# Input, convolution and recurrence of one channel tile after another, and other places for early weights

## The chip, the cores and the metric

The kernel runs on one core of a Trainium2 chip. Its engines are TensorE (PE, with its weight loads PEld), VectorE (DVE), ScalarE (ACT), GpSimd (POOL) and SyncE (SP), which issues most DMAs. The metric is the device time of one execution in microseconds; lower is better.

## The reference, cut to what matters

One layer over 1024 latent tokens with a prefix of 256 context tokens, width 1024, all in float32.

1. adaLN: `silu(c) @ w_ada + b_ada` gives shift, scale and gate of two sublayers (for the context from `c_ctx`). `w_ada` is 1024 x 6144, 24 MB.
2. Mixer: `h = modulate(rmsnorm(x))` for latent and context tokens; one input projection with `w_in`, whose columns are q (512), k (128), v (128), the recurrence's input xr (512) and its gate branch gr (512). Group A is windowed attention with context keys. Group B is a recurrence:

```
xc = conv_b + sum_j conv_w[j] * shift(xr, j)        # width 4, latent and context apart
for d in (forward, backward):
    r, i = sigmoid(blockdiag(xc, w_r[d])), sigmoid(blockdiag(xc, w_i[d]))
    a = exp(-8 * r * softplus(-lam[d]));  b = sqrt(1 - a*a) * i * xc
    h_c = scan(a, b) over the context, from 0;  h_l = scan over the latent, from h_c's end
rnn = (h_l of both directions summed) * gelu(gr)
```

   Both groups go through `w_out`, then a gated residual.
3. A mixture of 16 experts, each of which picks 128 of the 1024 latent tokens, then a gated residual.

## The kernel before

A float32 operand is split into a high part (ScalarE copy) and the remainder (VectorE subtraction), and each product is made of three matmuls: high by high, high by remainder, remainder by high. The remainder and high part of `h` lie in SBUF as HH, HL (latent, 64 KB per partition) and CH_, CL_ (context, 16 KB).

The order of instructions is the program's, changed by a planner: it goes through the program in order of priority, places what its own cost estimates say is ready, and fills the waits of an engine with later work. The order on each engine is fixed when the kernel is built; each engine then works through its own list, with semaphores between them. Pools on the two sides of SBUF are stacks: a pool that opens after another has closed takes its space, and each tile waits only for the tiles that it overlaps.

The part that matters here, lines 208 to 624, runs in this order:

- Two context tiles of x are loaded (`load_x`), then the first third of w_ada (eight loads of 1 MB, `ada_load`, line 222): five into a ring of staging buffers, three more as slots come free, with two latent x tiles queued between. `ada_rows` (line 229) multiplies each with the conditioning vectors, four matmuls per MB. The columns of scale and shift follow (`ada_columns`), then the context's h.
- `kv_proj` makes k and v of one token tile (24 matmuls of 256 columns) with k and v's weights (`wkv`, split by `split_group`), first for the two context tiles.
- The recurrence's input has four channel tiles, 3 to 0 in order of use (`xr_weights`, line 271, splits one tile's weights; `projT`, line 281, runs them). Tile 3 is made for context and the first latent half together, then for the second half; k and v of the latent tiles stand between. The other 16 MB of w_ada are consumed by 16 calls of `ada_step` spread over these projections, through a ring of three slots; each step loads the next MB.
- Tiles 2, 1, 0 are made for the context (`xr_ctx`, line 479), the gates of adaLN are finished (`ada_gates`), and the space of CH_, CL_ and the staging goes to the recurrence's tiles.
- `conv(3)`, then for tiles 2, 1, 0 the latent projection (`xr_lat`, line 550; 48 matmuls of 512 columns) and its convolution (`conv`, line 457). `conv(t)` writes over the raw input of tile t+1.
- q's rotary tables (`rope_tables`), the router's weights and bias. Then `lru_tile` (line 508) for t = 3, 2, 1, 0: four gate products with block-diagonal weights (`gate_weights`, line 499: zeroed by VectorE, filled by four DMAs issued on POOL), tanh, exp, sqrt on ScalarE, products and three scans on VectorE. The gate tiles have four buffers, so that one tile's gates wait for the scans of the one before. Between the tiles stand five, five, five and one of the 16 steps of the query projection (24 matmuls of 256 columns each).
- The gate branch: for t = 3 to 0, 48 matmuls, gelu into a tile that lies in the recurrence's space, a product. k is stacked and transposed (`k_stack`), the eight query blocks are normalized and rotated (`norm_rope`), and attention starts (`q_stack`, `scores`).

## Time and profile before

| what | value |
|---|---|
| median of three runs | 1176.04 us (1173.61 to 1178.04) |
| the profiled execution | 1175.78 us, span 1174.0 us |
| TensorE, VectorE, ScalarE busy | 92%, 80%, 67% of the span |
| mean granted TensorE clock | 0.967 |

Times inside the profile are us from the span's start. A TensorE record lasts longer than its share of the array, because matmuls are pipelined and their ends are modelled: the distance from one start to the next is the better measure of what one costs. A granted clock of 1.00 is 2.4 GHz, and 0.50 is 1.2 GHz; values between are means over a stretch.

### The profile page before, as it was taken

The page shows a single profiled execution, that of the slowest core. Times are in us where ns is not written, and L with a number is a line of the kernel's source. Part 1 is how long each engine was busy: PE and PEld are TensorE (multiplying, and loading weights), DVE is VectorE, ACT ScalarE, POOL GpSimd, SP SyncE. Part 2 cuts the span into 40 slices and gives each one's busy share as a digit, 9 for nine tenths or more (in the row PEclk, how much of TensorE's full clock was granted, in tenths as well). Part 3 has the DMA queues.
Part 4 walks back from the last instruction along what each step waited for, and adds up shares of the span by engine and source line. Part 5 has one row for each costly group of instructions (what it writes and reads, how often), then busy time and mean ns, then how long its engine had stood idle before and what let it go on. Part 6 is the DMA issues. An engine that isn't in the chain of part 4 may idle for free.

```text
span 1174.0 us, 17069 instructions
## 1 busy us (share of the span) xinstructions
PE 1085.7 (92%) x6218; PEld 863.7 (74%) x6218; DVE 933.8 (80%) x1550; ACT 789.0 (67%) x1154; POOL 157.7 (13%) x226
## 2 busy tenths in 40 slices
PE   3999899899799999998299999999999999999995
PEld 0777678677678888786278888888888888877774
DVE  2537655778785585968888999999999999988885
ACT  2643137674475666664188888888888888897873
POOL 3015301110310000000100111101111101110001
PEclk9799899999899999999599999999999999999998
DMA  9886310102221112118799999999999999999932
GB/s 360 294 281 235 103 36 10 36 1 72 65 77 55 55 55 90 55 55 302 300 330 356 353 380 390 398 389 388 378 387 387 399 388 385 383 372 352 365 88 36
DMA packets 75636, 277.10 MB, mean 236 GB/s; under 512 B 5556, under 2 KB 12976, under 8 KB 72480
## 3 DMA queue, kind: packets, MB, share of 16 engines
q1 hardware_dynamic: 69056, 255.87, 57.3%
q0 software_dynamic: 6320, 20.07, 7.0%
q8 instruction: 49, 0.80, 0.3%
q14 instruction: 35, 0.29, 0.1%
q10 hardware_dynamic: 176, 0.07, 0.0%
HBM read 259.21 MB, written 16.79 MB: 235 GB/s over the span
## 4 chain that ended last, share of the span: by engine, by line
PE 68%; DVE 14%; ACT 7%; issue 5%; DMA 4%; POOL 2%; POOLq 0%; SPq 0%; ACTq 0%; DVEq 0%
PE pu L96 14%; PE pg L96 14%; PE pd L96 13%; PE py L96 7%; PE pxr L96 4%; PE pav L737 3%; PE pscore L96 3%; PE pPT L727 3%; DVE mlo L1090 2%; DMA wada<-in_w_ada_dram 2%; ACT gate L91 2%; PE pproj L96 1%; POOL rs L180 1%; PE pT L1131 1%; DVE gate L538 1%
## 5 line engine op out<-in xcount | busy, mean ns | idle before, releaser
L1090 DVE TENSOR_TENSOR mlo<-mraw,mhi 128x1024 fp32r<-128x1024 f32 x384 | 448.3, 1219 | 22.6 <-ACT mhi L1087 20.8
L1087 ACT ACTIVATE mhi<-mraw 128x1024 fp32r<-128x1024 f32 x384 | 397.5, 1063 | 74.2 <-PE pg L96 30.1
L96 PE MATMUL pg<-mlo,xsh 128*128 128x512 f32 x256 | 81.3, 398 | 1.4 <-DVE mlo L1090 1.4
L96 PE MATMUL pu<-mlo,xsh 128*128 128x512 f32 x256 | 80.2, 394 | 0.8 <-DVE mlo L1090 0.5
L96 PE MATMUL pu<-mhi,xsh 128*128 128x512 f32 x256 | 80.8, 390 | 0.0
L96 PE MATMUL pg<-mhi,xsh 128*128 128x512 f32 x256 | 80.5, 395 | 0.3 <-ACT xsh L1141 0.3
L96 PE MATMUL pg<-mhi,xsl 128*128 128x512 f32 x256 | 79.6, 391 | 0.0
L96 PE MATMUL pu<-mhi,xsl 128*128 128x512 f32 x256 | 79.0, 390 | 0.0
L96 PE MATMUL pd<-mlo,hdh 128*128 128x512 f32 x240 | 76.0, 398 | 2.4 <-DVE mlo L1090 2.4
L96 PE MATMUL pd<-mhi,hdh 128*128 128x512 f32 x240 | 76.4, 399 | 0.0
L96 PE MATMUL pd<-mhi,hdl 128*128 128x512 f32 x240 | 74.2, 391 | 0.0
L1118 POOL DMA_INDIRECT xs<-xh_dram,idx x16 | 22.1, 1380 | 371.5 <-ACT mhi L1087 336.5
L1180 POOL DMA_INDIRECT out_dram<-ys,idx x16 | 49.8, 3112 | 164.1 <-DVE ys L1178 164.1
L1140 ACT ACTIVATE xs<-pT,gcol 128x128 f32<-128x128 f32 x124 | 46.7, 460 | 27.1 <-PE pT L1131 27.1
L91 ACT ACTIVATE sc<-sc,mx 128x641 f32<-128x641 f32 (+1 forms) x64 | 50.9, 797 | 15.8 <-DVE mx L701 15.8
L96 PE MATMUL pproj<-wlo,hh 128*128 128x256 f32 x192 | 55.1, 287 | 4.4 <-DVE wlo L269 4.4
L701 DVE CUSTOM_DVE_ANT_0 sc<-pscore,kn,nsink 128x640 f32<-128x640 f32 (+1 forms) x64 | 53.4, 843 | 6.2 <-PE pscore L96 6.1
L96 PE MATMUL pproj<-whi,hh 128*128 128x256 f32 x192 | 57.4, 300 | 0.6 <-ACT gate L91 0.6
L96 PEld LDWEIGHTS pu<-mlo,xsh 128*128 128x128 f32 x256 | 47.1, 188 | 12.7 <-DVE mlo L1090 3.5
L733 ACT ACTIVATE pt<-pPT 128x512 f32<-128x512 f32 (+1 forms) x88 | 44.0, 534 | 18.1 <-PE pPT L727 17.0
L96 PEld LDWEIGHTS pg<-mlo,xsh 128*128 128x128 f32 x256 | 45.9, 188 | 13.4 <-DVE mlo L1090 5.4
L96 PE MATMUL py<-woh,mh 128*128 128x512 f32 x128 | 54.3, 425 | 1.4 <-DVE y L779 0.8
(339 smaller groups left out, 2414.1 us busy)
## 6 DMA issues: line engine op xcount, KB each, us to landing
mraw<-in_w_gate_dram SPq DMA_DIRECT2D x64, 1024.0 KB, 7.9
mraw<-in_w_up_dram SPq DMA_DIRECT2D x64, 1024.0 KB, 9.1
mraw<-in_w_down_dram SPq DMA_DIRECT2D x63, 1024.0 KB, 8.9
wada<-in_w_ada_dram SPq DMA_DIRECT2D x24, 1024.0 KB, 6.8
win<-in_w_in_dram SPq DMA_DIRECT2D x7, 1024.0 KB, 6.4
xa<-in_x_dram SPq DMA_DIRECT2D x8, 512.0 KB, 3.7
out_dram<-xa SPq DMA_DIRECT2D x8, 512.0 KB, 2.6
xh_dram<-xb SPq DMA_DIRECT2D x8, 512.0 KB, 2.9
```

The costliest lines, as they stand in the source:

```text
L91: i = nc.scalar.activation(*a, **kw)
L96: nc.tensor.matmul(o, l, r, start=start, stop=stop)
L180: nc.gpsimd.tensor_tensor(o, r, neghalf[:, :n], op=OP.pow)
L701: nc.vector.tensor_tensor_reduce(out=sb[:, :ntot], in0=ps[:, n0:n0 + ntot], in1=mk, scale=-0.125, scalar=nsink[:, h:h + 1], op0=OP.add, op ...
L727: nc.tensor.transpose(p[:, 2 * j + s, :], pe[s][:, (j0 + j) * 128:(j0 + j + 1) * 128], ident)
L733: nc.scalar.activation(dst, src, AF.Copy)
L737: nc.tensor.matmul(po[s * 64:(s + 1) * 64, :], V[:, kt, kv * 64:(kv + 1) * 64], pt[:, j, s], start=(j == 0), stop=(j == nk - 1), skip_grou ...
L1087: nc.scalar.activation(hi, raw[:, j], AF.Copy)
L1090: nc.vector.tensor_tensor(lo, raw[:, j], hi, op=OP.subtract)
L1118: g = nc.gpsimd.indirect_dma_start(out=xs, out_offset=None, in_=xh_dram, in_offset=bass.IndirectOffsetOnAxis(ap=idx[:, :1], axis=0))
L1140: nc.scalar.activation(xf[:, k], p[:, i], AF.Identity, scale=A_, bias=B_)
L1180: nc.gpsimd.indirect_dma_start(out=out_rows, out_offset=bass.IndirectOffsetOnAxis(ap=idx[:, :1], axis=0), in_=ys, in_offset=None, compute_ ...
```

## The change

- The eight loads of the first third of w_ada go into a pool of eight buffers of their own, which lies where HH and HL come later, and are issued at once. Only the other 16 MB use the ring of three.
- The weights of k and v are loaded into the tiles V and Kn, which hold v and k later, as five and three of the eight row blocks, and split in three pieces. The two buffers for w_in then hold the recurrence's inputs (`rx`, `rx10`), both loaded early.
- x tiles 2 to 5 are staged in the latent part of the recurrence's buffers and no longer at their start, and the squares' unused output goes to one of them, so that the context part is free.
- `xr_ctx` comes first, for tiles 3, 2, then (behind the first half of h) 1, 0; then k and v of the context. Tile 3's weights are split a second time for the latent part. Two ada steps instead of one follow each of the kv projections 2 to 5.
- `conv(3)` moves ahead of the last kv projections. Then come `lru_tile(3)`, the input and convolution of tile 2, the input of tile 1, `lru_tile(2)`, the convolution of tile 1, the input of tile 0, three query steps, `lru_tile(1)`, the convolution of tile 0, five query steps, `lru_tile(0)`, eight query steps, and q's rotary tables.

```diff
--- before.py
+++ after.py
@@ -207,22 +207,18 @@
 
     praw = pool(top, "raw", 2, "right")
     phl = pool(S_hl, "hilo", 3, "right")
-    ph = pool(S_h, "hT", 1, "right")
-    HH = ph.tile([128, KT, S], F32R, name="hh")
-    HL = ph.tile([128, KT, S], F32R, name="hl")
-    phc = pool(S_hc, "hTc", 1, "right")
-    CH_ = phc.tile([128, KT, NCTX], F32R, name="ch")
-    CL_ = phc.tile([128, KT, NCTX], F32R, name="cl")
-    paw = pool(S_aw, "adaw", 1, "right")
-
-
-    aring = [rq[0], rq[1], paw, praw, praw]
+    S_a8 = ExitStack()
+    pa8 = pool(S_a8, "ada8", KT, "right")
+
+
     nada = [0]
 
     def ada_load(g, k):
-        i = nada[0]
-        nada[0] += 1
-        w = aring[i if i < 5 else (i - 5) % 3].tile([128, 2048], F32, name="wada", tag="raw")
+        if g == 0:
+            w = pa8.tile([128, 2048], F32, name="wada", tag="raw")
+        else:
+            w = (rq[0], rq[1], paw)[nada[0] % 3].tile([128, 2048], F32, name="wada", tag="raw")
+            nada[0] += 1
         nc.sync.dma_start(w, w_ada[k * 128:(k + 1) * 128, g * 2048:(g + 1) * 2048])
         return w
 
@@ -276,7 +272,6 @@
         return split_w(raw[:, :, (t % 2) * 128:(t % 2 + 1) * 128], [128, KT, 128])
 
     CTX, LAT0, LAT1 = "ctx", "lat0", "lat1"
-    SEG = {CTX: (CH_, CL_, 0, 256), LAT0: (HH, HL, 0, 512), LAT1: (HH, HL, 512, 512)}
 
     def projT(hi, lo, segs, between={}):
 
@@ -297,7 +292,7 @@
     def load_x(ti):
 
         if 2 <= ti < 6:
-            xt = XR[(0, 1, 2, 4)[ti - 2]][:, 0:D]
+            xt = XR[(0, 1, 2, 4)[ti - 2]][:, XL0 + 2:XL0 + 2 + D]
         else:
             xt = a0x.tile([128, D], F32, name="xt")
         srcd = ctx_d[ti * 128:(ti + 1) * 128] if ti < 2 else x_d[(ti - 2) * 128:(ti - 1) * 128]
@@ -305,26 +300,37 @@
         return xt
 
     def xhat(xt, ti):
-        junk = V[:, 2:10].rearrange("p a b -> p (a b)") if ti < 6 else XR[4][:, 0:D]
+        junk = XR[3 if ti < 6 else 4][:, XL0 + 2:XL0 + 2 + D]
         nc.scalar.activation(junk, xt, AF.Square, accum_out=ss[:, ti:ti + 1])
         rs = rstd_of(a0, ss[:, ti:ti + 1], 1, D, "rs1")
         nc.vector.tensor_scalar(xt, xt, rs, None, op0=OP.mult)
 
     xs = [load_x(i) for i in range(2)]
-    wa = [ada_load(0, k) for k in range(5)]
+    wa = [ada_load(0, k) for k in range(KT)]
+    rx = load_raw(768 + 256)
     xs += [load_x(i) for i in range(2, 4)]
+
+    w_kv = w_in[:, 512:768].rearrange("(k p) c -> p k c", p=128)
+    rkv = [V.rearrange("p (k a) b -> p k (a b)", a=2), Kn[:, 0:6].rearrange("p (k a) b -> p k (a b)", a=2)]
+    nc.sync.dma_start(rkv[0], w_kv[:, 0:5])
+    nc.sync.dma_start(rkv[1], w_kv[:, 5:8])
+    xs += [load_x(i) for i in range(4, 6)]
+    rx10 = load_raw(768)
+    xl = [load_x(i) for i in range(6, 8)]
     pa0 = pO("pada")
     for k in range(KT):
-        if k >= 5:
-            wa.append(ada_load(0, k))
         ada_rows(pa0, wa[k], k)
+    S_a8.close()
+    ph = pool(S_h, "hT", 1, "right")
+    HH = ph.tile([128, KT, S], F32R, name="hh")
+    HL = ph.tile([128, KT, S], F32R, name="hl")
+    paw = pool(S_aw, "adaw", 1, "right")
+    phc = pool(S_hc, "hTc", 1, "right")
+    CH_ = phc.tile([128, KT, NCTX], F32R, name="ch")
+    CL_ = phc.tile([128, KT, NCTX], F32R, name="cl")
+    SEG = {CTX: (CH_, CL_, 0, 256), LAT0: (HH, HL, 0, 512), LAT1: (HH, HL, 512, 512)}
     for i in range(4):
         xhat(xs[i], i)
-    rkv = load_raw(512)
-    xs += [load_x(i) for i in range(4, 6)]
-    rx = load_raw(768 + 256)
-    xl = [load_x(i) for i in range(6, 8)]
-    wkv = split_group(rkv)
 
     pad = ada_columns(pa0, slice(0, 2))
     bb = sm[:, off["b_ada"]:off["b_ada"] + 16].rearrange("p (j t) -> p j t", j=4)
@@ -379,6 +385,18 @@
         hilo_of(hf, CH_[:, k:k + 2].rearrange("p a b -> p (a b)"), CL_[:, k:k + 2].rearrange("p a b -> p (a b)"), k // 2)
     for i in range(4, 6):
         xhat(xs[i], i)
+    for a, b in ((0, 2), (NCTX + 2, NCTX + 5), (NT + 5, NT + 6)):
+        nc.vector.memset(XR0[:, a:b], 0.0)
+        nc.vector.memset(XR14[:, 0:3, a:b], 0.0)
+
+    def xr_ctx(t, raw):
+        hl = xr_weights(raw, t)
+        po = pO("pxrc")[:, :NCTX]
+        projT(hl[0], hl[1], [(po, CTX)])
+        nc.scalar.activation(XR[t][:, XC0 + 2:XC0 + 2 + NCTX], po, AF.Copy)
+
+    xr_ctx(3, rx)
+    xr_ctx(2, rx)
     xl += [load_x(i) for i in range(8, 10)]
     po12 = pS("pada")
     order = [(g, k) for k in range(KT) for g in (1, 2)]
@@ -389,22 +407,30 @@
         g, k = order[nstep[0]]
         nstep[0] += 1
         ada_rows(po12[:, (g - 1) * 512:g * 512], wa.pop(0), k)
-        if nada[0] < 24:
-            wa.append(ada_load(*order[nada[0] - 8]))
-
+        if nada[0] < 16:
+            wa.append(ada_load(*order[nada[0]]))
+
+    h_lat(xs[2:6], 0)
+    xr_ctx(1, rx10)
+    xr_ctx(0, rx10)
+    wkv = []
+    for parts in (((0, 4, rkv[0], 0),), ((0, 1, rkv[0], 4), (1, 3, rkv[1], 0))):
+        hi = phl.tile([128, 4, 256], F32R, name="whi")
+        lo = phl.tile([128, 4, 256], F32R, name="wlo")
+        for k, n, raw, k0 in parts:
+            nc.scalar.activation(hi[:, k:k + n], raw[:, k0:k0 + n], AF.Copy)
+            nc.vector.tensor_tensor(lo[:, k:k + n], raw[:, k0:k0 + n], hi[:, k:k + n], op=OP.subtract)
+        wkv.append((hi, lo))
     for tt in range(2):
         kv_proj(tt)
+    S_hc.close()
     w3 = xr_weights(rx, 3)
-    h_lat(xs[2:6], 0)
-    xr3 = pS("pxr")
-    projT(w3[0], w3[1], [(xr3[:, 512:768], CTX), (xr3[:, 0:512], LAT0)], {2: ada_step, 4: ada_step, 6: ada_step})
-    for a, b in ((0, 2), (NCTX + 2, NCTX + 5), (NT + 5, NT + 6)):
-        nc.vector.memset(XR0[:, a:b], 0.0)
-        nc.vector.memset(XR14[:, 0:3, a:b], 0.0)
-    nc.scalar.activation(XR[3][:, XC0 + 2:XC0 + 2 + NCTX], xr3[:, 512:768], AF.Copy)
-    nc.scalar.activation(XR[3][:, XL0 + 2:XL0 + 514], xr3[:, 0:512], AF.Copy)
+    po = pO("pxr3")
+    projT(w3[0], w3[1], [(po, LAT0)], {3: ada_step, 6: ada_step})
+    nc.scalar.activation(XR[3][:, XL0 + 2:XL0 + 514], po, AF.Copy)
     for tt in range(2, 6):
         kv_proj(tt)
+        ada_step()
         ada_step()
     for i in range(4):
         xhat(xl[i], 6 + i)
@@ -466,27 +492,17 @@
                                                    op0=OP.mult, op1=OP.add)
         return i
 
-    po = pO("pxr1")
+    po = pO("pxr3")
     projT(w3[0], w3[1], [(po, LAT1)], {3: ada_step, 6: ada_step})
     nc.scalar.activation(XR[3][:, XL0 + 514:XL0 + 1026], po, AF.Copy)
-    rx10 = load_raw(768)
+    conv(3)
     for tt in range(6, 10):
         kv_proj(tt)
         ada_step()
     for tt in range(10):
         norm_rope(Kn[:, tt].rearrange("p (h d) -> p h d", h=2), 2, tt - 2 if tt >= 2 else None, ktab)
-
-    def xr_ctx(t, hl):
-        po = pO("pxrc")[:, :NCTX]
-        projT(hl[0], hl[1], [(po, CTX)])
-        nc.scalar.activation(XR[t][:, XC0 + 2:XC0 + 2 + NCTX], po, AF.Copy)
-
-    for t, raw in ((2, rx), (1, rx10), (0, rx10)):
-        xr_ctx(t, xr_weights(raw, t))
-        ada_step()
     ada_gates(po12)
     S_aw.close()
-    S_hc.close()
     QBQ = [p_.tile([128, 4, 512], F32, name="qb", tag="raw") for p_ in rq]
     QB = [QBQ[b // 4][:, b % 4] for b in range(NB)]
     S_ropek.close()
@@ -553,12 +569,6 @@
         projT(hl[0], hl[1], [(ps[:, 0:512], LAT0), (ps[:, 512:1024], LAT1)])
         nc.scalar.activation(XR[t][:, XL0 + 2:XL0 + 2 + S], ps, AF.Copy)
 
-    conv(3)
-    for t, raw in ((2, rx), (1, rx10), (0, rx10)):
-        xr_lat(t, raw)
-        conv_end = conv(t)
-
-    qtab = rope_tables("q_norm_g", conv_end)
 
     wr = prope.tile([128, KT, NE], F32, name="wr", bufs=1)
     nc.gpsimd.dma_start(wr, A["w_router"][0].rearrange("(k p) e -> p k e", p=128))
@@ -571,13 +581,31 @@
     nc.vector.tensor_tensor(wrg[:, :, 0:NE], wr, gcol[:, 32:40, None].to_broadcast([128, KT, NE]), op=OP.mult)
 
     qsteps = [(g, b) for g in range(2) for b in range(NB)]
-    for i, t in enumerate((3, 2, 1, 0)):
-        lru_tile(t)
-        for g, b in qsteps[5 * i:5 * i + 5]:
+
+    def q_steps(n):
+        nonlocal wg
+        for _ in range(n):
+            g, b = qsteps.pop(0)
             if b == 0:
                 wg = split_group(load_raw(g * 256))
             po = proj(wg, b + 2)
             nc.scalar.activation(QB[b][:, g * 256:(g + 1) * 256], po, AF.Copy)
+
+    wg = None
+    lru_tile(3)
+    xr_lat(2, rx)
+    conv(2)
+    xr_lat(1, rx10)
+    lru_tile(2)
+    conv(1)
+    xr_lat(0, rx10)
+    q_steps(3)
+    lru_tile(1)
+    conv_end = conv(0)
+    q_steps(5)
+    lru_tile(0)
+    q_steps(8)
+    qtab = rope_tables("q_norm_g", conv_end)
 
     S_lru.close()
```

## Rows read from the trace of the kernel before

**Rows 1.** Busy times by stage: PE, PEld, DVE, ACT, POOL, then granted clock, DMA share, GB/s.

```profile
32.00:122.00 90.00, 88.05 (x604) 66.05 (x600) 50.54 (x120) 45.13 (x91) 22.28 (x36) 0.93 0.72 254
122.00:134.00 12.00, 8.20 (x34) 6.78 (x31) 7.50 (x14) 0.35 (x2) 2.68 (x4) 0.72 0.83 227
134.00:164.00 30.00, 30.00 (x136) 24.76 (x135) 14.91 (x22) 4.36 (x5) 5.92 (x10) 1.00 0.14 45
164.00:284.00 120.00, 109.75 (x603) 85.92 (x602) 89.12 (x81) 81.08 (x94) 14.14 (x17) 0.98 0.07 21
284.00:312.00 28.00, 24.56 (x107) 19.82 (x105) 20.52 (x34) 7.60 (x13) 11.98 (x18) 0.93 0.14 50
```

**Rows 2.** Chain of waits, start and length in us; then TensorE's timeline around one tile's gates.

```profile
64.64 2.88 PE pproj L96 x24
67.52 0.99 PE pada L231 x8
134.97 29.05 PE pxr L96 x128
...
165.55 0.68 PE L96 MATMUL pgatec<-xr,wg 128*128 128x256 f32 x2
...
173.84 0.68 PE L96 MATMUL pproj<-whi,hh 128*128 128x256 f32 x1
```

**Rows 3.** TensorE's timeline: behind the ada steps, behind the gate branch, the first scores.

```profile
122.03 0.72 PE L96 MATMUL pxr<-hh,whi 128*128 128x512 f32 x2
...
307.10 1.06 PE L597 MATMUL pT<-ident,xr 128*128 128x128 f32 x8
...
315.69 0.58 PE L96 MATMUL pscore<-kh,qst 128*128 128x256 f32 x1 [2.37 <-DVE qst L669]
```

**Rows 4.** What TensorE waited for, 32 to 318 us: total, times, longest.

```profile
PE pproj L96 <- DVE wlo L269: 5.0, 2, 4.4
PE pT L96 <- DVE adaev L237: 4.7, 2, 3.8
PE pT L597 <- DVE kl L600: 3.4, 1, 3.4
...
PE pgr L96 <- ACT ge L91: 2.0, 1, 2.0
```

**Rows 5.** Timelines of ScalarE and VectorE: first and last tile's gates, last sum of the recurrence.

```profile
166.27 0.47 ACT L91 ACTIVATE gate<-pgatec,hb 128x256 f32<-128x256 f32 x1 [0.70 <-PE pgatec L96]
...
250.18 0.47 ACT L91 ACTIVATE gate<-pgatec,hb 128x256 f32<-128x256 f32 x1
...
281.90 1.22 DVE L548 TENSOR_TENSOR xr<-gate 128x1024 f32<-128x1024 f32 x1
```

**Rows 6.** TensorE's timeline at the last load of w_ada's first third; busy times of 20 to 30 us.

```profile
30.41 1.93 PE L231 MATMUL pada<-wada,cst 128*32 128x512 f32 x8 [0.58 <-DMA wada<-in_w_ada_dram]
...
20.00:30.00 10.00, 4.93 (x24) 0.56 (x24) 1.51 (x2) 2.30 (x4) 1.76 (x4) 0.71 1.01 415
```

**Rows 7.** ScalarE's splits in 32 to 122 us; VectorE's split and convolution of one tile.

```profile
L267 ACT ACTIVATE whi<-win 128x1024 fp32r<-128x1024 f32 x9 | 9.4, 1055 | 5.3 <-PE pxrc L96 3.8 <-PE pxr L96 1.5
...
142.93 1.23 DVE L269 TENSOR_TENSOR wlo<-win,whi 128x1024 fp32r<-128x1024 f32 x1 [5.09 <-ACT whi L267]
144.07 0.81 DVE L462 TENSOR_SCALAR xr<-xr,sm 128x1024 f32<-128x1024 f32 x1
144.91 3.93 DVE L465 SCALAR_TENSOR_TENSOR xr<-xr,sm 128x1024 f32<-128x1024 f32 x3
```

**Rows 8.** Tile view of w_ada's buffers, 42 to 122 us: from issue to landing.

```profile
DMA to landing us min/median/max: 4.8/5.1/11.2
```

**Rows 9.** Timelines of VectorE and POOL; tile view of the block weights.

```profile
126.29 0.68 DVE L237 COPY adaev<-pada 128x512 f32<-128x512 f32 x1
...
139.24 1.19 POOL L505 DMA_DIRECT2D wg<-in_lru_w_i_dram  x2
...
DMA to landing us min/median/max: 2.0/2.1/2.2
```

## Prediction

> **What bounds the kernel now.** I cut the span into stages, followed the chain of waits through 0 to 330 us (the part that the diff touches), and listed what TensorE waits for there. The reader is to see first that TensorE is busy 88 of 90 us from 32 to 122, all of 134 to 164, and 109.75 of 120 from 164 to 284, while VectorE has 14.9 of 30 and then 89 of 120 [rows 1]. So TensorE sets the pace; VectorE and ScalarE come forward only from 164, in the recurrence.
>
> Busy time hides how much room there is, since matmuls overlap in the record. I count by starts instead: 24 matmuls of 256 columns follow each other in 2.88 us, 128 of 512 columns in 29.05 us (0.227 each), and one channel tile's gates take 165.55 to 173.84, 8.3 us [rows 2]. From the end of the last ada step (122.0) to the end of the gate branch (307.1, [rows 3]) TensorE has: three latent inputs, 3 x 48 x 0.227 = 32.7; gates, 4 x 8.3 = 33.2; queries, 16 x 2.88 = 46.1; the gate branch, 4 x 48 x 0.227 = 43.6; the ada columns, the router bias and k's transposes, 6 by estimate from their few small matmuls. Sum 161.6 of 185.1 us: 23.5 us are lost, to waits [rows 4] and to the clock that falls after them (0.72 in 122 to 134, 0.93 in 284 to 312, [rows 1]). The busy column leaves 17.5 idle in 122 to 312 (190 less 172.5), some 4 of it after 307.1, so 14; with that loss in place of 23.5 the sum below would gain 9 us less. The Trainium skill, Perfetto Trace Analysis, section Identifying the Most-Contended Engine, holds matmul busy time a bad measure of headroom and asks for the weight loads' busy share. The starts in this trace agree with it.
>
> Why is it lost? The order runs all three latent inputs first (134 to 164, VectorE half idle), and only then the recurrence, whose four tiles are a chain: first gates at 166.27, the fourth tile's at 250.18, so 28 us per tile, and the last sum ends at 283.1 [rows 5]. The first scores come at 315.69 [rows 3], 32.6 us after the chain's end.
>
> **Part by part.**
>
> Staging of w_ada over h: the eight loads of the first group no longer wait for ring slots, and only the two context tiles stand ahead of them. Before, two x tiles (1.05 MB) were queued ahead of the last three loads, and the last was used from 30.41; at 415 GB/s 1.05 MB is 2.5 us [rows 6]. Gain 2.5, bounds 0 and 3. In exchange x tiles 2 to 5 come behind the group and behind w_in's first MB, and their four squares fall into ScalarE's busy stretch (two did before).
>
> k's weights over V and Kn, split in three pieces instead of two (same elements), and tile 3's weights split twice: one more ScalarE split of 1.055 and one VectorE split of 1.2 [rows 7]. ScalarE is busy 45 of 90 us there [rows 1] and covers it; without cover it is 2.3 us. With the squares I charge 1 us, bounds 0 and 5.
>
> Context inputs first: three projections of 2.88 move from behind the kv projections to before them; TensorE's work is the same. The ada steps go from 3+4+2+4+3 to 2+8+2+4. Two now follow each of four kv projections, 2.88 + 2 x 0.99 = 4.9 us for two steps [rows 2], so each of the three ring slots turns in 7.3. A step (1.0) and a landing (5.1 in the middle, 11.2 at most, [rows 8]) make 6.1: no wait. At 11.2 it would be 12.2, so 4.9 per three steps, 13 us over eight. I take 0, nearest the median, and give the 13 to a rival. On SyncE's queue w_in's second MB and k's two loads now pass ahead of the second ada group: 19 MB up to its third load, 48 us at 415 GB/s, while its first step now comes behind four context projections; nothing charged. The x tiles' shift by 259 columns and the moved zeroing cost nothing.
>
> So the last ada step ends at 122.0 - 2.5 + 1 = 120.5.
>
> The recurrence among the inputs. Its gates need the block-diagonal weights, whose space frees only after the ada columns. Before, the first column copy was at 126.29, POOL had issued the first tile's four loads by 140.4, and a landing takes 2.1 [rows 9]: 142.5, 16 after the copy. Now 121 + 16 = 137 for the first gates, 29 us earlier than 166.27. TensorE has two inputs (21.8 us) to run meanwhile. POOL has nothing else then; behind its wait for the zeroed tile stand only the next block weights. With the chain as long as before, 116.8, it ends at 254; plus 32.6, scores at 286: the earliest by this chain. If three convolutions (0.81 + 3.93 each) and three splits (1.2) all stand in it on VectorE [rows 7], it is 17.8 longer and scores come at 304.
>
> TensorE's own line: 120.5 + 161.6 + losses. Losses lie between 0 and the old 23.5. The 2.0 us for the gelu output goes with its slow clock (about 3): its space is the recurrence's, now free earlier. Waits of gates for ScalarE shrink, since inputs or queries can stand between. The wait for the ada columns (3.8, then slow clock) and that for the second query weights' remainder (4.4) may stay [rows 4]. I take 10, a little under half: the gate branch ends at 292.1. To the first scores it was 8.6 us, of which 3.4 was a wait for k's remainder behind query norms on VectorE [rows 4], which now has time earlier: 7.6. Scores at 299.7, later than 286, so TensorE bounds: 315.7 - 299.7 = 16.
>
> q's tables move behind the last recurrence tile: three DMAs on POOL behind the block weights and five VectorE instructions, none longer than a split (1.2, so at most 6 us), needed when the first query block is whole. Cover: TensorE's 43.6 us of gate branch; without it up to 6.
>
> After the scores nothing changes, so 16 us come off the end. The profiled execution took 1175.8 (span 1174.0), 0.3 under the median of three, 1176.04: 1160.
>
> **Rivals.**
>
> *Slower: TensorE stands before the gates.* Matmuls don't overtake: TensorE stood 4.4 us for one weight remainder with gates behind it [rows 4]. The program now names tile 3's gates ahead of the inputs. If the planner puts them so on TensorE, it stands from 121 to 137, 16 us, and 5 again before tile 0, where five queries (14.4) and gates (8.3) fall short of 28; each gap brings about 3 us of slow clock. With the 10 of other losses the gate branch ends at 120.5 + 161.6 + 37 = 319.1, scores at 326.7: 1187. It decides from 22 us of added standing on. Against it: the planner places what is ready by its estimates, and after the ada steps an input is ready and the gates are not. The Trainium skill, TensorE: Matmul & The Clock Gate, section Architectural detail, says that the queue pulls only weight loads ahead. By that rule this rival has its full price where the order is so. Chance 0.12.
>
> *The w_ada ring starves.* Two loads are in flight all the time, and at the longest landing 13 us and 3 of slow clock eat the gain; at two thirds of it 1170 (1164 to 1177). Against: no step of the second group waited for its load before. Chance 0.13.
>
> *It does not do what it says: inputs still run first*, since the gates' weights come late. Then the chain starts at 120.5 + 32.7 + 4 = 157, 9 us earlier than before, and goes on as before: 1167. Within 3 us of it lies the chain stretched by its full 17.8 (scores 304: 1164). Chance 0.13.
>
> **How the numbers follow.** Forecast 0.62, its own range 1149 to 1169 (losses 0 to 20). A measurement here tells about 0.5%, 5.9 us. Faster: 0.61 + 0.07 + 0.10 = 0.78; within: 0.01 + 0.06 + 0.03 = 0.10; slower 0.12. The range 1148 to 1175 leaves out the slower rival and the ends of the others.
>
> **What would show it.** The first group's last w_ada used near 28; last ada step near 120; first gates near 137 with input matmuls before them and no TensorE gap over 5 us from 120 to 140; the recurrence's end at 254 to 270; the gate branch's near 292; first scores near 300; the rest as long as before. It is wrong if ada matmuls wait for loads, if TensorE stands before the gates, or if the stretch after the first scores changes.

## The result and the profile after

The changed kernel took 1184.67 us (median of five, 1183.59 to 1187.95) beside 1176.04 for the kernel before: a ratio of 1.0071, 95% interval 1.0053 to 1.0088. It is 8 us slower, clear of noise; 16 us faster was forecast. The profiled execution took 1184.67 (span 1182.9), with a mean granted clock of 0.957 (before 0.967).

Busy times by stage, the stretches of [rows 1], columns as there:

```profile
32.00:122.00 90.00, 85.48 (x595) 63.74 (x595) 49.48 (x98) 45.31 (x90) 19.01 (x31) 0.95 0.74 266
122.00:134.00 12.00, 3.21 (x15) 3.13 (x15) 9.40 (x35) 3.15 (x7) 3.85 (x9) 0.65 0.02 5
134.00:164.00 30.00, 24.43 (x83) 17.14 (x84) 6.73 (x17) 13.29 (x14) 11.68 (x18) 0.74 0.25 70
164.00:284.00 120.00, 114.00 (x633) 92.51 (x632) 90.63 (x78) 70.47 (x83) 11.23 (x11) 0.97 0.09 28
284.00:312.00 28.00, 28.00 (x126) 23.09 (x125) 19.40 (x34) 7.45 (x10) 10.77 (x10) 1.00 0.12 38
```

From 284 to 312 TensorE is full at full clock, and from 164 to 284 it is 4 us busier than before, though one loss still lies there (below). Most of the loss is between 122 and 164. From 122 to 134 TensorE works 3.2 of 12 us (8.2 before), and from 134 to 164 it has a clock of 0.74 (1.00 before). TensorE's timeline of that stretch, and of the later places that answer to [rows 3, 6] (start, length, what it runs, in brackets the idle time before it and its releaser):

```profile
27.94 1.94 PE L227 MATMUL pada<-wada,cst 128*32 128x512 f32 x8 [0.61 <-DMA wada<-in_w_ada_dram]
...
120.32 1.06 PE L227 MATMUL pada<-wada,cst 128*32 128x512 f32 x8
129.32 1.87 PE L96 MATMUL pT<-sel,adaev 128*128 128x4 f32 x8 [7.93 <-DVE adaev L233]
132.66 1.87 PE L96 MATMUL pT<-sel,adaev 128*128 128x4 f32 x8 [1.47 <-DVE adaev L233]
...
140.49 3.56 PE L96 MATMUL pbrow<-wr,gcol 128*128 128x16 f32 x16 [5.30 <-DMA wr<-in_w_router_dram]
143.89 1.20 PE L96 MATMUL pgatec<-xr,wg 128*128 128x256 f32 x2
144.88 3.62 PE L96 MATMUL pgate<-xr,wg 128*128 128x512 f32 x4
...
153.60 1.88 PE L96 MATMUL pgate<-xr,wg 128*128 128x512 f32 x4
154.92 1.03 PE L96 MATMUL pxr<-hh,whi 128*128 128x512 f32 x2
...
177.12 1.03 PE L96 MATMUL pgatec<-xr,wg 128*128 128x256 f32 x4
182.90 5.70 PE L96 MATMUL pgate<-xr,wg 128*128 128x512 f32 x8 [4.75 <-DVE xr L491]
...
192.33 1.03 PE L96 MATMUL pxr<-hh,whi 128*128 128x512 f32 x2
...
313.45 0.61 PE L96 MATMUL pgr<-hh,wlo 128*128 128x512 f32 x2
...
322.25 0.58 PE L96 MATMUL pscore<-kh,qst 128*128 128x256 f32 x1 [3.04 <-DVE qst L697]
```

After the last ada step no input follows. TensorE stands for the ada columns, then for the router's weights, then runs the gates of tile 3 at half clock (3.62 us for four matmuls that take 1.88 at full clock), and the first latent input starts only at 154.92. From the end of the last ada step (121.38) to there it is 33.5 us. They hold 8.3 of gates and 3.4 of columns and bias (by their starts where TensorE is not kept waiting, in the seventh run below): 21.8 are lost. The gates of tile 2 take 15.2 (177.12 to 192.33) for 8.3, because they wait for the convolution of tile 2 (4.75 us) and part of them runs at a slow clock: another 6.9. The whole loss up to the end of the gate branch is 314.06 - 121.38 - 161.6 = 31.1 us; it was 23.5, and 10 were forecast. The first scores come at 322.25 in place of 315.69, and from there to the end it takes 860.7 us (858.3 before).

What kept the columns and the gates' weights, in VectorE's and GpSimd's timelines (beside [rows 9] and the last sum of [rows 5]):

```profile
124.18 0.29 DVE L468 TENSOR_TENSOR kn<-kn,rs 128x128 f32<-128x128 f32 x1 [0.59 <-POOL rs L180]
...
128.58 0.68 DVE L233 COPY adaev<-pada 128x512 f32<-128x512 f32 x1
...
131.92 0.68 DVE L233 COPY adaev<-pada 128x512 f32<-128x512 f32 x1
...
270.83 1.22 DVE L564 TENSOR_TENSOR xr<-gate 128x1024 f32<-128x1024 f32 x1
```

```profile
130.55 0.70 POOL L180 TENSOR_TENSOR rs<-rs_r,neghalf 128x2 f32<-128x2 f32 x1
135.79 1.16 POOL L252 DMA_DIRECT2D row_dram<-grow  x2 [4.54 <-DVE grow L250]
136.98 0.93 POOL L574 DMA_DIRECT2D wr<-in_w_router_dram  x1
...
142.06 1.24 POOL L521 DMA_DIRECT2D wg<-in_lru_w_i_dram  x2
```

VectorE copies the ada columns behind k's norms, each of which goes to GpSimd and back (`rs`); the fifth run, with the norms named later, shows that this is what held the copies (first copy at 122.4 in place of 128.6). In the old order three context projections stood between the last k projection and the last ada step; in the new one the k projections run up to it, so the norms fall where the copies are wanted. GpSimd stores the columns' rows only when they are there (135.79, after 4.54 us of waiting), and its loads of the router's and then of the gates' weights stand behind that in its queue.

### The profile page after: what moved, and what is told of

Read it like the earlier page. It is cut to its first block, busy times and chain, and to the rows that moved or that the text cites. A ratio compares the mean times of both kernels' runs of the same rounds, so it can differ in the third digit from the quotient of the medians.

```text
span 1182.9 us, 17060 instructions
## 1 busy us (share of the span) xinstructions
PE 1087.5 (92%) x6218; PEld 866.3 (73%) x6218; DVE 932.5 (79%) x1552; ACT 791.9 (67%) x1156; POOL 158.3 (13%) x226
## 4 chain that ended last, share of the span: by engine, by line
PE 69%; DVE 14%; ACT 5%; issue 4%; DMA 4%; POOL 3%; POOLq 0%; ACTq 0%; SPq 0%; DVEq 0%
PE pu L96 14%; PE pg L96 13%; PE pd L96 13%; PE py L96 7%; PE pav L765 3%; PE pscore L96 3%; PE pPT L755 3%; DVE mlo L1118 2%; PE pproj L96 2%; PE pgate L96 2%; DMA wada<-in_w_ada_dram 2%; POOL rs L180 2%; PE pxr L96 1%; ACT gate L91 1%; PE pT L1159 1%
## 5 line engine op out<-in xcount | busy, mean ns | idle before, releaser
L1146 POOL DMA_INDIRECT xs<-xh_dram,idx x16 | 21.8, 1366 | 371.7 <-ACT mhi L1115 336.8
L761 ACT ACTIVATE pt<-pPT 128x512 f32<-128x512 f32 (+1 forms) x88 | 44.0, 533 | 19.6 <-PE pPT L755 18.5
L96 PEld LDWEIGHTS pg<-mhi,xsl 128*128 128x128 f32 x256 | 48.0, 188 | 10.4
```

The lines of the kernel that those rows point to most:

```text
L96: nc.tensor.matmul(o, l, r, start=start, stop=stop)
L761: nc.scalar.activation(dst, src, AF.Copy)
L1146: g = nc.gpsimd.indirect_dma_start(out=xs, out_offset=None, in_=xh_dram, in_offset=bass.IndirectOffsetOnAxis(ap=idx[:, :1], axis=0))
```

## Experiments

They change the order of the program, the PSUM buffers of some sums, or the engine of two copies; none leaves out work. PSUM is the memory in which TensorE's sums build up. The loss is computed as above (end of the gate branch less end of the last ada step less 161.6); times are those of the profiled executions, ratios are to the kernel before on the same chip.

| run | ratio (95%) | first gates | loss | first scores |
|---|---|---|---|---|
| before | 1 | 165.6 | 23.5 | 315.7 |
| the change | 1.0071 (1.0053 to 1.0088) | 143.9 | 31.1 | 322.3 |
| 1 inputs 2, 1 first | 1.0068 (1.0045 to 1.0092) | 157.8 | 29.9 | 322.8 |
| 2 input 2 in two PSUM buffers | 0.9992 (0.9973 to 1.0011) | 148.1 | 20.7 | 313.8 |
| 3 early half alone | 1.0030 (1.0009 to 1.0050) | 167.5 | 25.9 | 317.6 |
| 4 late half alone | 1.0035 (1.0018 to 1.0052) | 140.6 | 26.9 | 317.8 |
| 5 k norms late | 1.0021 (1.0011 to 1.0032) | 135.3 | 24.1 | 316.2 |
| 6 input 2 first | 0.9987 (0.9970 to 1.0004) | 147.1 | 19.6 | 312.5 |
| 7 both of 5 and 6 | 0.9921 (0.9894 to 0.9947) | 138.2 | 13.1 | 306.4 |
| 8 as 7, copies on ScalarE | 0.9923 (0.9901 to 0.9946) | 136.6 | 12.6 | 304.2 |
| 9 as 8, queries 2/3/6/5 | 0.9945 (0.9929 to 0.9962) | 138.6 | 19.5 | 311.8 |
| 10 as 8, queries 3/3/6/4 | 0.9986 (0.9974 to 0.9998) | 138.4 | 23.4 | 315.6 |
| 11 router late | 1.0092 (1.0060 to 1.0125) | 143.6 | 34.9 | 325.5 |
| 12 as 3, k norms late | 1.0002 (0.9990 to 1.0013) | 158.6 | 21.0 | 314.9 |
| 13 as 8, input 0 in the transposes' PSUM buffers | 0.9891 (0.9872 to 0.9910) | 136.4 | 9.6 | 301.0 |
| 14 as 8, order of the change, all inputs in the transposes' PSUM buffers | 1.0010 (0.9993 to 1.0028) | 137.7 | 23.0 | 314.2 |

**1. Inputs of tiles 2 and 1 ahead of the recurrence of tile 3.**

```diff
-    lru_tile(3)
     xr_lat(2, rx)
-    conv(2)
     xr_lat(1, rx10)
+    lru_tile(3)
+    conv(2)
     lru_tile(2)
```

> The changed kernel with two lines moved: the latent inputs of tiles 2 and 1 are named ahead of the recurrence of tile 3. Order theory (in the changed kernel TensorE stands from 121 to 144 us, because the gates of tile 3 are ahead of every input and both 1024-column PSUM buffers go to them in program order): inputs run from 121 on, no TensorE gap over 5 us from 121 to 143, first gates 144 to 148 as in the changed kernel, the loss up to the end of the gate branch goes from 31 to 10 to 16 us, the gate branch ends at 294 to 300, time 1166 to 1172. Rival, VectorE's backlog (the copies of the ada columns come 8 us late behind k's norms and everything after is late by it): the gates come as late as now and the time stays above 1180. Rival, the early part (context first, two steps per projection) costs by itself: above 1180 too.

Measured: 1.0068, no gain. The time is that of the rivals (above 1180), and the first gates come at 157.8 and not at 144 to 148; but TensorE's timeline shows the stand (time in which TensorE waits) in a place that none of the three named:

```profile
131.03 1.87 PE L96 MATMUL pT<-sel,adaev 128*128 128x4 f32 x8 [6.15 <-DVE adaev L233]
...
157.78 0.60 PE L96 MATMUL pgatec<-xr,wg 128*128 128x256 f32 x2
...
186.31 1.22 PE L96 MATMUL pgatec<-xr,wg 128*128 128x256 f32 x2 [15.46 <-ACT gate L91]
```

The inputs do run before the gates, but then the third gate of tile 2 waits for a gate buffer, 28.5 us behind the first of tile 3. What is left, input 0 and the queries, is named behind it, and none of it was put into the wait. So the result neither clears nor damns the order; it says that an input is wanted both ahead of the gates of tile 3 and behind them. Sixth run: one each.

**2. Program order of the change, input 2 in PSUM buffers that the gates don't use.** The pool of 1024-column buffers has two. In the change one holds the ada sums until they are copied, and both then go, in program order, to the four gate products of tile 3 before input 2.

```diff
     def xr_lat(t, raw):
         hl = xr_weights(raw, t)
+        if t == 2:
+            for n, (p, sg) in enumerate(((pT("pxr2"), LAT0), (pT("pxr2"), LAT1))):
+                p = p.rearrange("p a b -> p (a b)")
+                projT(hl[0], hl[1], [(p, sg)])
+                c0 = XL0 + 2 + n * 512
+                nc.scalar.activation(XR[t][:, c0:c0 + 512], p, AF.Copy)
+            return
         ps = pS("pxr")
```

> The changed kernel in its own program order; only the latent input of tile 2 is summed in two 512-column buffers of the transposes' PSUM pool and no longer in one 1024-column buffer of the pool that the gates use. Buffer theory (the planner would have run the input in the gap, but its PSUM buffer is the third in line behind two gate products): some 30 of the 48 matmuls now stand ahead of the first gate, the input begins at 133 to 136 right behind the transposed columns instead of at 154.9, 7 to 11 us and part of the slow clock come back, the gate branch ends at 302 to 307, time 1173 to 1178. Rival, the planner prefers gates by program order whatever is free, or the gates' weights set the pace: no gain, 1183 to 1187.

Measured: 0.9992, 9 us less than the change (0.0079 of 1176), inside the buffer theory's range. The input starts 1.6 us later than expected, behind the transposed columns. TensorE's timeline:

```profile
137.64 0.78 PE L96 MATMUL pxr<-hh,whi 128*128 128x512 f32 x1
...
147.88 0.40 PE L96 MATMUL pxr<-hh,whi 128*128 128x512 f32 x1
148.12 0.60 PE L96 MATMUL pgatec<-xr,wg 128*128 128x256 f32 x2
```

With not a line of the program's order changed, input 2 now fills the stretch ahead of the gates. The buffer was what kept it behind. The Trainium skill, Perfetto Trace Analysis, section Optimization Strategy, says of a gap that repeats for a stretch, on the engine that should be saturated, that too little SBUF or PSUM for the next tile can be behind it. Here the gap came once and did not repeat; that a PSUM buffer was behind it is what this run shows, with 9 us.

**3 and 4. Each half of the change alone.** The early half is the changed kernel with the old order from the ada columns on; the late half is the kernel before with the new order there (in both, the block between the router's weights and `S_lru.close()`, and the loop of `xr_lat` and `conv`, are the other kernel's).

> The early half of the change alone (w_ada's first group over h, context inputs first, k's weights over V and Kn, two ada steps per projection, the third convolution early), and from the ada columns on the order of before: all latent inputs, then the four recurrences with five, five, five and one query steps. Order theory: the early part costs nothing, the last ada step ends near 121 and all that follows is as before, so 0 to 3 us faster than before: 1172 to 1177. Rival, the early part costs by itself (ScalarE's and VectorE's extra splits, the ring): 1181 or more.

> The late half of the change alone: the early part of before, and behind the ada columns the new order (recurrence of tile 3, input 2, input 1, recurrence 2, input 0, three queries and so on). Order theory: TensorE stands before the gates here too, 15 to 25 us of standing and slow clock against 10 us saved later, so slower than before by 6 to 14 us: 1182 to 1190. Rival, the early part is what costs: without it the new order gives its gain, 1160 to 1172.

Measured: 1.0030 and 1.0035, which add up to the change's 1.0071 within their intervals. So the late half is slower by itself, as the order theory has it, though by 4 us and not by 6 to 14; and the early half is not free, against both theories' numbers (3.5 us, between them). Its wait for the columns is 6.8 us at the longest, against 3.8 [rows 4]:

```profile
PE pT L96 <- DVE adaev L233: 6.8, 1, 6.8
```

The late half's waits (engine, tile and line, releaser; total, times, longest):

```profile
PE pgatec L96 <- DMA wg<-in_lru_w_r_dram: 6.4, 1, 6.4
PE pT L96 <- DVE adaev L237: 5.8, 2, 4.9
```

It stands for the gates' weights themselves: with the norms done earlier, and the router's weights there in time, the gates are still ahead of every input.

**5. k's norms behind the recurrence of tile 3.** Here and in the runs built on it the tables of k's norms stay open until the recurrence ends, and the norms' temporaries are those of q's pool.

```diff
-    for tt in range(10):
-        norm_rope(Kn[:, tt]...)
     ada_gates(po12)
...
     lru_tile(3)
+    for tt in range(10):
+        norm_rope(Kn[:, tt]...)
```

> The changed kernel in its own order of inputs and recurrences; only the ten k norms are named behind the recurrence of tile 3 and no longer ahead of the ada columns. Backlog theory (half of the standing before the gates is VectorE's and GpSimd's: the k norms, which now end at 134 because the k projections end last, delay the copies of the ada columns by 7 us and the loads of the block weights with them): the copies come at 121 to 123, the first gates at 134 to 138 in place of 143.9, time 1174 to 1179. Order theory alone: TensorE still stands before the gates, they come a little earlier, and the norms' 18 us on VectorE stretch the recurrence and give it back: 1181 to 1186.

Measured: 1.0021, 6 us less than the change, inside the backlog theory's range (median 1178.65). First gates at 135.3; the wait for the columns is gone, that for the router's weights is not, and the convolution's has grown:

```profile
PE pgate L96 <- DVE xr L491: 8.0, 1, 8.0
PE pbrow L96 <- DMA wr<-in_w_router_dram: 5.1, 1, 5.1
...
PE pT L96 <- DVE adaev L233: 2.6, 3, 0.9
```

**6. Input 2 alone ahead of the recurrence of tile 3.**

```diff
-    lru_tile(3)
     xr_lat(2, rx)
+    lru_tile(3)
```

> The changed kernel with one line moved: the latent input of tile 2 alone ahead of the recurrence of tile 3 (in the run with inputs 2 and 1 ahead, nothing was left to run between the gates of tiles 3 and 2, and TensorE stood 15.5 us there). Order theory with that correction: a stand of 6 us for the ada columns stays (VectorE), then the input up to 144, gates of tile 3 at 144 to 146 without standing, input 1, gates of tile 2 with 0 to 5 us of standing; loss up to the end of the gate branch 13 to 20 us in place of 31, time 1167 to 1175. Rival, the recurrence's chain is what counts (first gates no earlier than in the changed kernel): 1181 or more.

Measured: 0.9987, 10 us less than the change; the median, 1175.25, is just above the range. It is about the gain of the PSUM buffers (9 us), by another way. The stand for the columns, 6.3 us, stays:

```profile
123.14 0.72 PE L96 MATMUL pxr<-hh,whi 128*128 128x512 f32 x2
...
131.36 1.87 PE L96 MATMUL pT<-sel,adaev 128*128 128x4 f32 x8 [6.34 <-DVE adaev L233]
```

The first line shows that the weights and operands of input 2 were ready when the ada steps ended (123.2 here). Seven of its matmuls run, then come the transposes of the columns, for which TensorE waits with the other matmuls of the input behind them.

**7 and 8. Order and norms together; then the copies on ScalarE** (`nc.scalar.activation(ev, po, AF.Copy)` in `ada_columns` for the two copies of `ada_gates`).

> Both: the latent input of tile 2 ahead of the recurrence of tile 3, and the ten k norms behind it. If order and VectorE's backlog are the whole cause, TensorE has no gap over 3 us from 121 to 150, the first gates come at 134 to 140, the loss up to the end of the gate branch is 6 to 12 us and the time 1160 to 1168, what was forecast for the change. If the forecast's sum was wrong in itself (its losses later, or the part after the scores): no better than the run with the order alone, 1168 or more.

> The same, and the two copies of the ada columns on ScalarE, which has nothing to do there. If VectorE's queue still holds the copies back after the k norms are gone, 1 to 3 us faster than the run with both; if not, within 1 us of it.

Measured: 0.9921 and 0.9923 (medians 1169.74 and 1167.04), 18 us less than the change and 9 less than before. The fifth and sixth runs gained 6 and 10 by themselves, so the two causes add up. The copies' engine makes no difference that these runs tell. Of the stages in the seventh run:

```profile
122.00:134.00 12.00, 12.00 (x67) 9.36 (x67) 5.84 (x12) 2.45 (x7) 4.28 (x7) 1.00 0.37 98
134.00:164.00 30.00, 28.41 (x112) 19.31 (x110) 21.39 (x52) 19.96 (x24) 19.23 (x26) 1.00 0.11 31
```

TensorE has no gap after the ada steps and its clock does not fall; the first gates come at 138.2 and 136.6, where 137 was forecast; the loss is 13.1 and 12.6, where 10 was. The median of the seventh is 2 us above its range, and its loss 1 us, though it is 5.5 us under the order alone. What is left is one stand, 6.5 us, at the third gate of tile 2 (from the eighth run's timeline):

```profile
167.29 1.22 PE L96 MATMUL pgatec<-xr,wg 128*128 128x256 f32 x2 [6.46 <-ACT gate L91]
```

**9 and 10. Query steps into that stand.**

```diff
     xr_lat(1, rx10)
+    q_steps(2)
     lru_tile(2)
...
-    q_steps(5)
+    q_steps(6)
     lru_tile(0)
-    q_steps(8)
+    q_steps(5)
```

(The tenth has 3, 3, 6 and 4.)

> The run with input 2 first, late k norms and the columns copied by ScalarE, and its query steps handed out as two, three, six and five behind the inputs 1 and 0 and the gates of tiles 1 and 0 (before: none, three, five, eight). There TensorE stood 6.5 us between the gates of tiles 3 and 2, at a granted clock of 0.88, with only input 1 (10.9 us) to run. Two query steps are 5.8 us: the stand goes, with 2 to 3 us of slow clock, and no other comes: 1158 to 1163. If the recurrence's chain bounds there (28.5 us per tile) and TensorE has its gap later, between tiles 1 and 0 or ahead of the gate branch: within 2 us of that run, 1165 to 1169.

> The same with three, three, six and four query steps: 8.6 us between the gates of tiles 3 and 2, more than the stand of 6.5. If the stand is all that is left there, as with two steps or 1 us better (1157 to 1163); if TensorE's extra step makes the chain start late, 1 to 3 us worse than with two.

Measured: 0.9945 and 0.9986, worse than the eighth by 3 us (within the two intervals) and by 7 us (beyond them): both expectations missed. The stand fell to 2.3 and 2.8 us, but the gates came later: the first ones of tile 2 moved from 156.1 to 163.8 and 166.5, and the fourth tile's last gates from 226.7 to 244.7 and 251.3. The waits of the ninth:

```profile
PE pgatec L96 <- ACT gate L91: 4.8, 2, 2.5
PE pproj L96 <- DVE wlo L268: 3.5, 1, 3.5
PE pxr L96 <- DVE wlo L268: 2.2, 1, 2.2
```

Two new waits are for weight remainders on VectorE, in a queue that the recurrence fills. Of the ninth run's delay of 7.7 us at tile 2's first gates, 2.0 are there at its last ada step (123.9 against 121.9); the other 5.7 are the two query steps (2 x 2.88), so work put ahead of the gates delays them by its full length. Another 10 us come behind these gates. There the edit has six query steps between tiles 1 and 0 in place of five, and the wait for the second query weights' remainder, 4.4 before [rows 4], is back (3.5; 6.2 in the tenth); with the change's three and five it was gone. How much of the loss is the new place and how much the other counts, these two runs don't separate. The thirteenth run puts work behind the first two gates, which have their buffers, and not ahead of them.

**11. The router's weights and bias behind the queries** (the block from `wr =` to `wrg[...]` moved).

> The changed kernel with the router's weights, bias and scaled weights behind all query steps; inputs, recurrences and k norms as in the changed kernel. Order and backlog theory: the 5.3 us that the router bias waited for its weights was no loss of its own, since the gates behind it had their block weights no earlier than 143 us: 0 to 3 us faster than the changed kernel, 1181 to 1185. Rival, the late load of the router's weights is what held the gates: 5 us and some slow clock come back, 1175 to 1179.

Measured: 1.0092, first gates at 143.6. The 5.3 us that the bias waited was no loss of its own, as the first theory has it: without it TensorE stood for the gates' weights.

```profile
PE pgatec L96 <- DMA wg<-in_lru_w_r_dram: 6.6, 1, 6.6
```

The time is above both ranges (median 1187.6), but its interval overlaps that of the change.

**12. The early half with k's norms behind the three inputs.**

> The early half alone with the order of before behind it, which cost 3 us, and now the k norms behind the three latent inputs. Backlog theory: the 3 us were the ada columns' copy, 3 us later than before because the k projections, and with them k's norms, end 9 us nearer to the last ada step; with the norms away the stand of 6.8 us goes with its slow clock: 1170 to 1175, faster than before. Rival, the early half costs by itself: 1178 or more.

Measured: 1.0002. 3 us came back, not the 5 to 10 expected, so neither range holds it. The first gates come 9 us earlier than in the third run (158.6 against 167.5), but the last ones only 2.7 (253.2 against 255.9): from first to last gates it grew from 88.4 to 94.6 us. Most of that, 3.6, is in the first tile's gates. The router's bias waits to be copied by VectorE, behind k's norms, and the second gate waits for the PSUM buffer that the bias holds:

```profile
164.35 0.70 PE L96 MATMUL pgatec<-xr,wg 128*128 128x256 f32 x2 [3.35 <-DVE brow L584]
```

**13 and 14. The same PSUM buffers for input 0; then for all inputs, in the order of the change.**

> The run with input 2 first, late k norms and the columns copied by ScalarE (1167), and the latent input of tile 0 summed in two 512-column buffers of the transposes' pool in place of one that the gates use. Buffer theory: the planner now places 18 of its matmuls (4.1 us) between the second and the fourth gate of tile 2, where TensorE stood 6.5 us; the stand falls under 3 us with most of the slow clock behind it, the loss up to the end of the gate branch goes from 12.5 to 6 to 9 us, time 1160 to 1164. If the recurrence's chain sets the end there, the same stand comes later (tiles 1 or 0): 1165 to 1169.

> The changed kernel's order in the program (recurrence of tile 3 named ahead of every input) with late k norms and the columns copied by ScalarE, and all three latent inputs in two 512-column buffers of their own. Buffer theory: the inputs fill the waits by themselves; TensorE still stands some 4 us for the ada columns, whose transposes share the pool, then no gap over 3 us before the gates: 1161 to 1170. Rival, the order in the program is what decides: TensorE stands before the gates as in the run with late norms alone, 1176 to 1180.

Measured: 0.9891 for the thirteenth (median 1164.54, 1161.12 to 1165.81), the fastest of all, 13 us less than before and 4 less than the eighth, though these two intervals overlap a little. The median is 0.5 us above the buffer theory's range and the loss (9.6) 0.6 above its own, but under the other theory's 1165 to 1169, and no such stand comes later. Input 0 begins behind the second gate of tile 2, and the stand is halved:

```profile
158.67 1.98 PE L96 MATMUL pgate<-xr,wg 128*128 128x512 f32 x4
160.09 0.79 PE L96 MATMUL pxr<-hh,whi 128*128 128x512 f32 x1
...
167.13 1.22 PE L96 MATMUL pgatec<-xr,wg 128*128 128x256 f32 x2 [3.03 <-ACT gate L91]
...
301.01 0.58 PE L96 MATMUL pscore<-kh,qst 128*128 128x256 f32 x1 [2.59 <-DVE qst L707]
```

The fourteenth fails, 1.0010, against the buffer theory's 1161 to 1170. TensorE stands 2.1 us in all before the gates of tile 3, as that theory has it, but with all inputs free of the gates' buffers they were put between the gates of tile 2, whose fourth now comes at 182.57, 15 us behind the third (171.63 in the thirteenth run). The rival's time came out, by another way than its own:

```profile
167.53 0.70 PE L96 MATMUL pgatec<-xr,wg 128*128 128x256 f32 x2 [2.05 <-ACT gate L91]
...
182.57 0.59 PE L96 MATMUL pgatec<-xr,wg 128*128 128x256 f32 x2
```

So buffers decide what can fill a wait, and the order in the program still decides what does. Both must fit.

## Why the prediction was wrong, point by point

- **The early part** was right in its first step: the first group's last w_ada ran from 27.94 (30.41 before, [rows 6]; 28 forecast), and no ada step from 32 us on waited for its load: the ring did not starve. But the last ada step ended at 121.4 (120.5 forecast), and in the 14 profiles with the early half at 121.4 to 123.9, 122.3 in the middle, against 122.1 before: the forecast gain of 1.5 us did not reach the end of the ada steps. One of its effects was not seen. Moving the context projections ahead of the k projections costs TensorE nothing, but those projections had covered k's norms. The text let the wait for the columns "stay" at 3.8 us. Before, VectorE was in the third convolution and a split from 121.6 to 126.3, ahead of the first copy; the change moved that convolution away, and k's norms took its place: the wait grew to 7.9, and the third run prices the early half at 3.5 us instead of a gain of 1.5. With the norms late (twelfth run) it costs nothing and gains nothing.
- **The first gates.** "121 + 16 = 137" counts from the first column copy, and the 16 held (15.3, from 128.58 to 143.89). But it puts that copy at 121, right behind the last ada step, while before it came 4.2 us behind, and here 7.2. "POOL has nothing else then" was wrong too: k's norms run on it to 131, and the rows' stores and two other loads stand ahead of the gates' loads.
- **The step that failed** is "TensorE has two inputs (21.8 us) to run meanwhile". It had the first one's weights and operands (sixth run), but not a PSUM buffer (second run), and so it had nothing. This was the premise of taking 10 us of losses; they were 31.1, of which the seventh run, with input 2 ahead and the norms late, takes back 18. The slower rival, "TensorE stands before the gates", was dismissed with the same sentence in other words: that an input is ready after the ada steps and the gates are not.
- **The slower rival was right in mechanism and nearly in size.** It charged 16 us of standing and two slow-clock spells of 3 and a second gap of 5 before tile 0, 27 in all, and gave 1187; the losses in its two places are 21.8 and 6.9, 28.7 in all, and 1184.67 was measured. That the total comes so near is in part luck: it had 10 us of other losses where 2.4 are left, and nothing for k's norms, the router's weights or the buffers, which made the standing. Its second gap came before tile 2, whose convolution was late, and not before tile 0. Its chance was 0.12.
- **The sum itself comes out** where its premise holds, or nearly. In the thirteenth run the loss is 9.6 (10 forecast), the gate branch ends at 292.9 (292.1) and the first scores come at 301.0 (299.7); in the eighth it is 12.6, 296.1 and 304.2. But the 10 was a choice, "a little under half" of the old losses, and the thirteenth run has a buffer and late norms that the forecast did not have; that it meets the 10 is in part luck. The first gates come at 136 to 138 there (137).
- **The chain's length** was taken as 116.8 us from the first gates to the last sum, 17.8 more at worst. In the change it is 126.9 (first gates at 145.13 on ScalarE, last sum ended at 272.05): inside the bounds. The first scores came 50.2 us behind that sum, so it did not set the end. In the tenth run they came 38.2 behind it, and in the old order (before, third and twelfth runs) 32.5 to 32.6.
- **After the scores** 2.4 us were lost where none was charged: 860.7 against 858.3. The same stretch took 858.3 to 863.9 in the profiles of the runs, in kernels that differ only ahead of it. TensorE's idle time in it is 47 to 49 us in all of them; what differs is its busy time, 810 to 816 us for the same matmuls, at a mean granted clock of 0.98 (before) or 0.97. So it is not a new wait; why TensorE was slower was not tried.

## What to carry to other kernels

Before counting an operation as ready to fill a wait, list everything that it needs, its PSUM buffer too: a rotating pool hands its buffers out in program order, and one operation behind four others on a pool of two can't run in their wait. When work is moved, ask what it covered on other engines where it stood, as these projections covered k's norms. And filler for a wait in a chain such as this recurrence did better here behind the instructions that feed the chain (thirteenth run) than ahead of them, where it delayed them by its length (ninth).

## What was not expected of the hardware

The changed kernel and the first, second, sixth and eleventh runs have the same program up to the ada columns, and yet the last ada step ended at 121.4, 123.1, 123.4, 123.2 and 122.2: from 32 to 119 us the granted clock was 0.95 in the change and 0.90 to 0.91 in the other four. That is up to 2 us, nearly the 2.5 that was forecast for the staging, so one profile of each kernel does not show such a gain.

The stand before the gates cost more than its length. Stretches of the changed kernel, columns as in [rows 1]:

```profile
135.20:140.40 5.20, 0.00 (x0) 0.00 (x0) 1.25 (x3) 0.00 (x0) 4.57 (x8) 0.50 0.82 224
140.50:143.80 3.30, 3.30 (x16) 3.30 (x16) 0.24 (x1) 0.00 (x0) 3.30 (x6) 0.50 0.22 60
143.90:148.20 4.30, 4.30 (x7) 2.15 (x8) 0.24 (x2) 0.47 (x1) 1.20 (x2) 0.50 0.45 130
...
150.00:154.00 4.00, 4.00 (x12) 2.08 (x11) 1.49 (x1) 2.13 (x4) 0.00 (x0) 1.00 0.01 4
```

The granted clock had fallen to 0.50 (1.2 GHz) while TensorE stood, and the rows of the work behind it, the router's bias and the first gate (140.5 to 148.2), are at 0.50 too; by 150 it was back at 1.00 (2.4 GHz). In the seventh run, in which TensorE stands nowhere from 122 to 160, 122 to 164 has 1.00 throughout. The forecast had 3 us of slow clock per gap; here a bias of 1.7 us took 3.4 (140.49 to 143.89) and the first gate 4.4 (143.89 to 148.30) in place of 2.2, 3.9 us in all.
